# Expert weights of a mixture-of-experts block, read in runs of 4 KB a partition instead of 2 KB

## The chip, the core and the metric

One Trainium2 chip, and of it one core. The metric is the time of one execution on the device in microseconds (us); the kernel before takes 679.34 us in the median of three runs (679.24, 679.34 and 680.87). One further execution was profiled, and every row of a profile or trace in this text comes from that one.

## The reference

One layer of a hybrid encoder block on 512 tokens of width 1024, all in float32: a mixing part (attention and a state-space part), then a mixture of experts in two levels. The change lies in the second part:

```python
def hierarchical_moe(h, w_rg, b_rg, w_re, b_re, w1, w3, w2):
    ...
    for e in range(N_EXPERTS):                               # 16
        y_e = (jax.nn.silu(t @ w1[e]) * (t @ w3[e])) @ w2[e]
        out = out + combine[:, e:e + 1] * y_e
```

`w1[e]` and `w3[e]` are 1024 x 512, `w2[e]` is 512 x 1024, each 2 MB; the 48 matrices make 100.7 MB. `combine` is zero but for two experts a token, so an expert sees only its own tokens. Before the experts come the residual sum `x`, its norm and a router.

## The kernel before

**The mixing part** ends in a product with `w_out`, whose pieces `wt` are read, split into a high and a low half (ScalarE, VectorE) and multiplied into PSUM banks `px`. For each tile t of 128 tokens and each half nh of the width, VectorE adds the residual (`x2_add`, L1362), ScalarE squares it, TensorE turns it for the router, and `u_w` (L1400 to L1402) multiplies it by the norm's weights into `us`. `u_mul` scales `us` by 1/rms, and `h2_store` writes it to HBM as `h2_d`. Between the `u_w`s VectorE runs the router's top-k.

**The experts.** Each of 16 experts has 96 slots, in three rounds r of 32. The work goes in four quarters q: expert 4j+q has the 32-column strip j of TensorE, so that four experts run beside each other. A *group* is the four multiplies of one channel block k and one round r; each stands in the trace as two passes. The gathered tokens are turned to `TH` (channels on partitions); `up_mm` (L1671) multiplies eight blocks k of `w1` (phase "u") and of `w3` (phase "v"); `g_silu` (ScalarE) and `g_mul` (VectorE) make the gated product, `s_t` and `s_out` turn it, and `down_mm` (L1680) multiplies four blocks k of `w2`. The width of the result is done in two halves, phases "0" and "1", each with its own loads. `y_ev` weighs the result (VectorE for half 1, L1843), and GpSimd adds it to the output by an indirect DMA (`scatter`, L1709). In the last quarter the down groups go by r, then half, then k.

**The order.** `Plan` (L123) simulates the kernel on the host with a cost for each job, a due number (`prio`) and pools of buffers, and emits the instructions of each engine in the order that comes out; nothing is reordered on the chip. `phases` (L1739) sets the order of the experts' phases and loads.

**The loads.** All 192 come from the SP queue by `eload` (L1711), 512 KB each: two blocks k of one matrix of one expert, on 128 partitions. They go into 35 buffers, which `spent` gives back four at a time after the last round of a block pair. A load takes its channels as

```python
    w1v = w1[0].rearrange("e (k p) f -> e p k f", p=P)
```

so a partition holds channels p, 128 + p, ...: its two rows of a load lie apart in HBM, and each is a run of 512 x 4 B = 2 KB. A name such as 13_1_3 in a trace is half 1 of quarter 3, second pair of blocks, strip 3: it is the last load of all.

Of the kernel before, what the change touches and what calls it, by code (L numbers as in the profile page):

```python
# [15 lines left out]
AF = mybir.ActivationFunctionType  # L16
ALU = mybir.AluOpType
# [3 lines left out]
P = 128  # L21
# [7 lines left out]
DE = 512  # L29
# [185 lines left out]
def tile_block(ctx: ExitStack, tc: tile.TileContext, x, norm_mix_w, w_in, b_gate, q_norm_w, k_norm_w,  # L215
# [1179 lines left out]
    def u_rs(t):  # L1395
        tt = slice(t, t + 1)
        return [(0.07, lambda: V.scalar_tensor_tensor(ss2[:, tt], ssh[:, t, 0:1], EPS, ssh[:, t, 1:2], op0=ALU.add, op1=ALU.add))
                ] + rsqrt(rs2[:, tt], ss2[:, tt], 1, 0)

    def u_w(t, nh):  # L1400
        ns = slice(nh * 512, (nh + 1) * 512)
        V.tensor_tensor(us(t)[:, ns], x2(t)[:, ns], nfw()[:, ns], op=ALU.mult)  # L1402

    def u_mul(t):
        A.activation(us(t), us(t), AF.Copy, scale=rs2[:, t:t + 1])
# [172 lines left out]
    job("dve", 0.1, lambda: V.tensor_copy(cnt, t_["plt"][:, 144:160]), [j_, j_slot[NT - 1]], free=["ac"], prio=800)  # L1578


    w1v = w1[0].rearrange("e (k p) f -> e p k f", p=P)
    w3v = w3[0].rearrange("e (k p) f -> e p k f", p=P)
    w2v = w2[0].rearrange("e (k p) f -> e p k f", p=P)
    ohp = [cp.tile([P, NT, P], BF16, name="oh_%d" % i) for i in range(NR)]


# [93 lines left out]
    def down_mm(h, q, r, k, tag):  # L1680
        if k == 0:
            t_["p", h, q, r] = bank(tag, "py%s%d_%d" % (h, q, r))
        for j in range(4):
            js = slice(j * RN, (j + 1) * RN)
            T.matmul(t_["p", h, q, r][js, :], lhsT=sT_(r)[:, k, js], rhs=t_["raw", h, q, k // 2, j][:, k % 2, :],  # L1685
                     start=k == 0, stop=k == 3)

    def spent(x_, q, kk):

        for j in range(4):  # L1690
            t_.pop(("raw", x_, q, kk, j))
            ebufs.append(t_.pop(("buf", x_, q, kk, j), r4))

    def g_silu(q, r):
        A.activation(s_buf(r), t_["p", "u", q, r], AF.Silu)

    def g_mul(q, r):
        V.tensor_tensor(s_buf(r), s_buf(r), t_["p", "v", q, r], op=ALU.mult)  # L1698

    def s_t(q, r):  # L1700
        t_["ps", q, r] = bank("tp", "ps%d_%d" % (q, r))
# [14 lines left out]
    def source(x_, e, kk):  # L1716
        if x_ in "uv":
            return (w1v if x_ == "u" else w3v)[e][:, kk * 2:kk * 2 + 2, :]
        return w2v[e][:, kk * 2:kk * 2 + 2, int(x_) * 512:(int(x_) + 1) * 512]

    def more(make, nm, after):

# [12 lines left out]
    for i in range(2):  # L1735
        more(g8, "EXu%d" % i, j_h2[2 * i:2 * i + 2] + pgs)


    phases = [("u", 0), ("v", 0), ("u", 1), ("0", 0), ("1", 0), ("v", 1), ("u", 2), ("0", 1), ("1", 1), ("v", 2), ("u", 3),  # L1739
              ("0", 2), ("1", 2), ("v", 3), ("0", 3), ("1", 3)]  # L1740
    at = {ph: 2000 + 100 * i for i, ph in enumerate(phases)}
    jw, jT, jti, jsT, jy, jmul, jgx = {}, {}, {}, {}, {}, {}, {}
    for x_, q in phases:
        for kk in range(4 if x_ in "uv" else 2):
            for j in range(4):
                key = (x_, q, kk, j)
                jw[key] = last["e"] = job(
                    "dma", 1.38, lambda key=key: eload(key, source(key[0], 4 * key[3] + key[1], key[2])),
                    [j_rq] + ([last["e"]] if "e" in last else []), ["e"], prio=1000 + len(jw), lat=DLAT)

    def sl_jobs(q):
# [26 lines left out]

    def t_jobs(q):
        for r in range(NR):  # L1780
            o = (1900, at["v", 0] + 40 + 6 * r) [q] if q < 2 else at["0", q - 2] + 1 + r if r < 2 else at["v", q - 1] + 3
            jT[q, r] = []
            for kb in range(2):
                tk = ["T"] * (kb == 0)
                if (q, r) == (0, 0):
                    k_, free = pgj[kb], ["sc"]
                else:
                    k_ = [job("pe", 0.55, lambda r=r, kb=kb: t_mm(q, r, kb), [jgx[q, r]] + jT[q, r], ["tp"],
                              ["G"] if kb else [], prio=o + r, duty=0.5)]
                    free = ["tp"]  # L1790
                jT[q, r] = jT[q, r] + [job(
                    "dve" if kb else "act", 0.6 if kb else 0.48,
                    lambda r=r, kb=kb: t_out(q, r, kb, t_["pg", kb] if (q, r) == (0, 0) else t_["pg", q, r, kb]),
                    k_ + [j_rooms], tk, free, prio=o - 1500)]
# [24 lines left out]
                    jsT[q, r] = job("act", 0.48, lambda r=r: s_out(q, r), [k_], ["sT"], ["tp"], prio=p_)  # L1819
        return prev  # L1820

    def y_jobs(q, r, h, ks, tag, o, prev):
        end = ks[-1] == 3
        for k in ks:
            def f(k=k):
                down_mm(h, q, r, k, tag)
                if r == NR - 1 and k % 2:
                    spent(h, q, k // 2)
            prev = [job("pe", 0.857, f, [jw[h, q, k // 2, j] for j in range(4)] + [jsT[q, r]] + prev, [tag] if k == 0 else [],
                        (["e"] * 4 if r == NR - 1 and k % 2 else []) + (["sT"] if h == "1" and k == 3 else []), prio=o)]  # L1830
        if end:
            hi = int(h)
            jy[q, r, hi] = job("dve" if hi else "act", 0.6, lambda: y_ev(h, q, r, hi), prev + [jti[q][1]],
                               ["ys"] if hi == 0 else [], [tag], prio=o - 1500)
            if hi:
                k_ = job("pool", 1.03, lambda: scatter(q, r), [jy[q, r, 0], jy[q, r, 1]] + jsc[-1:], prio=o)
                jsc.append(job("dma", 1.3, lambda: None, [k_], free=["ys"], prio=-400, lat=6.0))
        return prev
# [14 lines left out]
    for x_, q in phases[2:]:  # L1853
        if x_ in "uv":
            prev = up_jobs(x_, q, prev)
        elif q < NQ - 1:
            tags = ("mm", "mm", "ac") if x_ == "1" else ("sc", "sc", "sc")
            for k in range(4):
                for r in range(NR):
                    prev = y_jobs(q, r, x_, [k], tags[r], at[x_, q] + k, prev)  # L1860
        elif x_ == "0":
            for r in range(NR):
                for h in "01":
                    prev = y_jobs(q, r, h, [0, 1, 2, 3], (("mm", "mm"), ("ac", "sc"), ("sc", "sc"))[r][int(h)], at["0", q] + 10 * r,
                                  prev)
    plan.run()
    order.close()

# [22 lines left out]
    def xround(e):  # L1891

        V.tensor_scalar(cur[:, 0:NT], cur[:, 0:NT], -float(CAP), None, op0=ALU.add)
        V.tensor_tensor(ohx, iota[:, :N].unsqueeze(1).to_broadcast([P, NT, N]),
                        cur[:, 0:NT].unsqueeze(2).to_broadcast([P, NT, N]), op=ALU.is_equal)
        pi = bank("ac", "pix")
        for t in range(NT):
            T.matmul(pi[:N, 0:5], lhsT=ohx[:, t, :], rhs=rcx[:, t, :], start=(t == 0), stop=(t == NT - 1))
        V.tensor_scalar(ixx[:N], pi[:N, 0:1], pi[:N, 1:2], None, op0=ALU.add)
        V.tensor_scalar(fxx[:N, 0:1], pi[:N, 0:1], pi[:N, 1:2], spare[:N, 0:1], op0=ALU.add, op1=ALU.subtract)  # L1900
        V.reduce_sum(fxx[:N, 1:2], pi[:N, 2:5], axis=AX.X)
        V.tensor_scalar(fxx[:N, 2:3], fxx[:N, 1:2], 0.0, None, op0=ALU.is_gt)
        V.tensor_tensor(fxx[:N, 0:1], fxx[:N, 0:1], fxx[:N, 2:3], op=ALU.mult)
        V.tensor_scalar(sxx[:N], fxx[:N, 0:1], spare[:N, 0:1], None, op0=ALU.add)
        g, tx, s_, sT, y_ = g_buf(0), T_(0, 0), s_buf(0), sT_(0), y_buf(0)
        gather(g[:N], ixx[:N, 0:1])

        def turn(src, dst, n, k0):
            pt = bank("tp", "ptx%d" % k0)
            for j in range(4):  # L1910
                T.transpose(pt[:, j * P:j * P + N], src[:N, (k0 + j) * P:(k0 + j + 1) * P], ident[:N, :N])
            A.activation(dst[:, k0:k0 + 4, :N], pt.rearrange(K4, k=4)[:, :, :N], AF.Copy)
        for k0 in (0, 4):
            turn(g, tx, N, k0)
        ex = [w[bass.ds(e, 1)].rearrange("o p k f -> p (o k) f") for w in (w1v, w3v, w2v)]

        def xpiece(nm, src):
            raw = r4(nm, F32, K8, k=2)
            nc.sync.dma_start(raw, src)
            return raw  # L1920

        def product(w_, lh, nk, cols, tag, nm):
            b_ = bank(tag, nm)
            for kk in range(nk // 2):
                raw = xpiece("%s_%d" % (nm, kk), w_[:, kk * 2:kk * 2 + 2, cols])
                for k in range(2):
                    T.matmul(b_[:N, :], lhsT=lh[:, kk * 2 + k, :N], rhs=raw[:, k, :], start=kk + k == 0,
                             stop=(kk + 1) * 2 == nk and k == 1)
            return b_
        A.activation(s_[:N], product(ex[0], tx, KD, slice(0, DE), "mm", "pux")[:N], AF.Silu)  # L1930
        V.tensor_tensor(s_[:N], s_[:N], product(ex[1], tx, KD, slice(0, DE), "mm", "pvx")[:N], op=ALU.mult)
        turn(s_, sT, N, 0)
        for h in range(2):
            hs = slice(h * 512, (h + 1) * 512)
            A.activation(y_[:N, hs], product(ex[2], sT, 4, hs, "sc", "pyx%d" % h)[:N], AF.Copy, scale=fxx[:N, 1:2])
        G.indirect_dma_start(out, bass.IndirectOffsetOnAxis(ap=sxx[:N, 0:1], axis=0), y_[:N], None, compute_op=ALU.add)
# [37 lines left out]
```

## Time and profile before

| | us |
|---|---|
| median of three runs | 679.34 |
| the profiled execution's own time | 680.03 |
| its span in the trace | 678.3 |
| first load of the experts issued | 270.68 |
| first multiply of the experts | 381.7 |
| first down group of the last quarter | 634.54 |
| last multiply ends (1.02 after 665.88) | 666.90 |

Times in the rows count from the span's start. Idle time stands in brackets behind an instruction, with what ended it. A busy TensorE is not one at its peak, since the ends of multiplies are modelled; its pace is read from the starts.

### The profile page before, as it was taken

The page shows a single profiled execution, that of the slowest core. Times are in us where ns is not written, and L with a number is a line of the kernel's source. Part 1 is how long each engine was busy: PE and PEld are TensorE (multiplying, and loading weights), DVE is VectorE, ACT ScalarE, POOL GpSimd, SP SyncE. Part 2 cuts the span into 40 slices and gives each one's busy share as a digit, 9 for nine tenths or more (in the row PEclk, how much of TensorE's full clock was granted, in tenths as well). Part 3 has the DMA queues.
Part 4 walks back from the last instruction along what each step waited for, and adds up shares of the span by engine and source line. Part 5 has one row for each costly group of instructions (what it writes and reads, how often), then busy time and mean ns, then how long its engine had stood idle before and what let it go on. Part 6 is the DMA issues. An engine that isn't in the chain of part 4 may idle for free. (4 is left out here: it accounts for less than half of the span.)

```text
span 678.3 us, 11450 instructions
## 1 busy us (share of the span) xinstructions
PE 653.3 (96%) x4635; PEld 396.6 (58%) x4637; DVE 321.2 (47%) x663; ACT 249.5 (37%) x450; POOL 84.2 (12%) x111
## 2 busy tenths in 40 slices
PE   7899999999999999999999999999999999999893
PEld 6788887777888888888877533323333333333220
DVE  4779868978699996666435731200110011001100
ACT  5535555777668778523435111111001100110100
POOL 4624100222000000000012110101200010001001
PEclk8999999999999999999999899999999999999997
DMA  8721733565221112997727959999999999999954
GB/s 283 192 75 42 178 94 71 155 180 128 61 63 35 30 33 66 279 359 258 268 103 277 345 174 386 390 388 390 364 340 388 388 363 337 388 386 363 340 143 64
DMA packets 104189, 155.37 MB, mean 229 GB/s; under 512 B 8569, under 2 KB 44933, under 8 KB 104133
## 3 DMA queue, kind: packets, MB, share of 16 engines
q1 hardware_dynamic: 95268, 131.79, 56.8%
q0 software_dynamic: 6800, 22.76, 12.8%
q8 instruction: 37, 0.61, 0.4%
q10 hardware_dynamic: 2064, 0.07, 0.2%
q14 instruction: 20, 0.16, 0.1%
HBM read 144.01 MB, written 10.58 MB: 228 GB/s over the span
## 5 line engine op out<-in xcount | busy, mean ns | idle before, releaser
L268 PE MATMUL b<-hTh,wc_hi 128*128 128x512 f32 x208 | 84.5, 406 | 0.0
L270 PE MATMUL b<-hTh,wc_lo 128*128 128x512 f32 x208 | 81.3, 391 | 0.0
L269 PE MATMUL b<-hTl,wc_hi 128*128 128x512 f32 x208 | 81.3, 391 | 0.0
L1677 PE MATMUL pu<-u,TH 128*32 128x512 f32 x528 | 63.8, 597 | 0.0
L1677 PE MATMUL pv<-v,TH 128*32 128x512 f32 x372 | 58.9, 593 | 0.0
L1843 DVE TENSOR_SCALAR YS<-py,ti 128x512 f32<-128x512 f32 x12 | 9.0, 751 | 89.4 <-PE py L1685 89.0
L1667 DVE COPY TH<-pg 128x512 f32<-128x512 f32 x12 | 8.3, 692 | 90.8 <-PE pg L1662 90.0
L1706 ACT ACTIVATE GS<-ps 128x512 f32<-128x512 f32 x12 | 7.0, 601 | 111.0 <-PE ps L1703 111.0
L663 ACT ACTIVATE wc_hi<-wc_r 128x1024 fp32r<-128x1024 f32 x34 | 36.0, 1059 | 29.3 <-PE b L269 22.2
L667 DVE TENSOR_TENSOR wc_lo<-wc_r,wc_hi 128x1024 fp32r<-128x1024 f32 x34 | 41.5, 1222 | 7.4 <-ACT wc_hi L663 7.3
L268 PEld LDWEIGHTS b<-hTh,wc_hi 128*128 128x128 f32 x208 | 39.1, 188 | 9.7 <-issue 1.5
L270 PEld LDWEIGHTS b<-hTh,wc_lo 128*128 128x128 f32 x208 | 39.0, 188 | 8.6
L269 PEld LDWEIGHTS b<-hTl,wc_hi 128*128 128x128 f32 x208 | 39.1, 188 | 7.1
L1677 PEld LDWEIGHTS pu<-u,TH 128*32 128x32 f32 x528 | 18.0, 111 | 38.8 <-issue 37.5
L1709 POOL DMA_INDIRECT out_dram<-YS,sx x12 | 18.7, 1562 | 145.0 <-DVE YS L1843 79.4
L1677 PEld LDWEIGHTS pv<-v,TH 128*32 128x32 f32 x372 | 15.4, 110 | 29.9 <-issue 29.8
L1677 PE MATMUL pv<-EXr,TH 128*32 128x512 f32 x96 | 32.7, 595 | 0.0
L1669 ACT ACTIVATE TH<-pg 128x512 f32<-128x512 f32 x12 | 7.2, 597 | 67.8 <-PE pg L1662 65.1
L1698 DVE TENSOR_TENSOR YS<-YS,pv 128x512 f32<-128x512 f32 x8 | 5.5, 689 | 46.0 <-PE pv L1677 46.0
L1677 PE MATMUL pv<-EXx,TH 128*32 128x512 f32 x120 | 26.8, 593 | 0.0
L1656 POOL DMA_INDIRECT GS<-h_d,ix x11 | 10.7, 970 | 122.0 <-PE pg L1662 111.9
L1163 DVE TENSOR_TENSOR PTl<-ppt,PTh 128x512 fp32r<-128x512 f32 x32 | 21.6, 687 | 4.4 <-ACT PTh L1158 4.2
(451 smaller groups left out, 1708.4 us busy)
## 6 DMA issues: line engine op xcount, KB each, us to landing
u<-in_w_dram SPq DMA_DIRECT2D x44, 512.0 KB
v<-in_w_dram SPq DMA_DIRECT2D x31, 512.0 KB
wc_r<-in_w_in_dram SPq DMA_DIRECT2D x26, 512.0 KB
EXx<-in_w_dram SPq DMA_DIRECT2D x20, 512.0 KB
EXr<-in_w_dram SPq DMA_DIRECT2D x20, 512.0 KB
EXu<-in_w_dram SPq DMA_DIRECT2D x20, 512.0 KB
EXm<-in_w_dram SPq DMA_DIRECT2D x10, 512.0 KB
x<-in_x_dram SPq DMA_DIRECT2D x8, 512.0 KB
```

The source lines that it names most:

```text
L268: T.matmul(ps, lhsT=lh, rhs=rh, start=first, stop=False)
L269: T.matmul(ps, lhsT=lh, rhs=rl, start=False, stop=False)
L270: T.matmul(ps, lhsT=ll, rhs=rh, start=False, stop=last)
L663: A.activation(t_["w", i][0], t_["raw", i], AF.Copy)
L667: V.tensor_tensor(l_, t_.pop(("raw", i)), h_.bitcast(F32), op=ALU.subtract)
L1163: V.tensor_tensor(PTl[:, :, q2], t_.pop(("pt", u)).rearrange("p (k q) -> p k q", k=NT), PTh[:, :, q2].bitcast(F32), op=ALU.subtract)
L1656: G.indirect_dma_start(g, None, h2_d, bass.IndirectOffsetOnAxis(ap=i, axis=0))
L1667: V.tensor_copy(o, i)
L1669: A.activation(o, i, AF.Copy)
L1677: T.matmul(t_["p", x_, q, r][js, :], lhsT=T_(q, r)[:, k, js], rhs=t_["raw", x_, q, k // 2, j][:, k % 2, :], start=k == 0, stop=k == KD - 1)
L1709: G.indirect_dma_start(out, bass.IndirectOffsetOnAxis(ap=sx[q][:, r:r + 1], axis=0), y_buf(r), None, compute_op=ALU.add)
L1843: V.tensor_scalar(o, i, w_, None, op0=ALU.mult)
```

## The change

The channels of `w1` and `w3`, and the gated products that `w2` takes, are numbered "(p k)" instead of "(k p)". A partition then holds neighbouring channels, and the two rows that it takes in one load are one run of 4 KB. To match, `u_w` writes the tokens' channels in the new order (its inputs are read eight elements, 32 B, apart), and `g_silu` and `g_mul` read their PSUM banks four elements (16 B) apart. The down loads take one block k of the full width of 1024 instead of two blocks of a half, so phases "0" and "1" become one phase "w", in which each block serves both halves. The planner's cost of a load is 1.29 instead of 1.38. The path for experts with more than 96 tokens, which the trace does not run, follows suit.

```diff
     def u_w(t, nh):
         ns = slice(nh * 512, (nh + 1) * 512)
-        V.tensor_tensor(us(t)[:, ns], x2(t)[:, ns], nfw()[:, ns], op=ALU.mult)
+        by_k = lambda a: a[:, ns].rearrange("n (p k) -> n k p", k=KD)
+        V.tensor_tensor(us(t).rearrange("n (k p) -> n k p", k=KD)[:, :, nh * 64:nh * 64 + 64], by_k(x2(t)), by_k(nfw()), op=ALU.mult)
...
-    w1v = w1[0].rearrange("e (k p) f -> e p k f", p=P)
-    w3v = w3[0].rearrange("e (k p) f -> e p k f", p=P)
-    w2v = w2[0].rearrange("e (k p) f -> e p k f", p=P)
+    w1v = w1[0].rearrange("e (p k) f -> e p k f", p=P)
+    w3v = w3[0].rearrange("e (p k) f -> e p k f", p=P)
+    w2v = w2[0].rearrange("e (p k) f -> e p k f", p=P)
...
-            T.matmul(t_["p", h, q, r][js, :], lhsT=sT_(r)[:, k, js], rhs=t_["raw", h, q, k // 2, j][:, k % 2, :],
+            T.matmul(t_["p", h, q, r][js, :], lhsT=sT_(r)[:, k, js],
+                     rhs=t_["raw", "w", q, k, j].rearrange("p a n -> p (a n)")[:, int(h) * 512:(int(h) + 1) * 512],
                      start=k == 0, stop=k == 3)
...
+    def by_k(a):
+        return a.rearrange("n (p k) -> n k p", k=4)
+
     def g_silu(q, r):
-        A.activation(s_buf(r), t_["p", "u", q, r], AF.Silu)
+        A.activation(s_buf(r).rearrange("n (k p) -> n k p", k=4), by_k(t_["p", "u", q, r]), AF.Silu)
 
     def g_mul(q, r):
-        V.tensor_tensor(s_buf(r), s_buf(r), t_["p", "v", q, r], op=ALU.mult)
+        s_ = s_buf(r).rearrange("n (k p) -> n k p", k=4)
+        V.tensor_tensor(s_, s_, by_k(t_["p", "v", q, r]), op=ALU.mult)
...
-        return w2v[e][:, kk * 2:kk * 2 + 2, int(x_) * 512:(int(x_) + 1) * 512]
+        return w2v[e][:, kk:kk + 1, :].rearrange("p k (a n) -> p (k a) n", a=2)
...
-    phases = [("u", 0), ("v", 0), ("u", 1), ("0", 0), ("1", 0), ("v", 1), ("u", 2), ("0", 1), ("1", 1), ("v", 2), ("u", 3),
-              ("0", 2), ("1", 2), ("v", 3), ("0", 3), ("1", 3)]
+    phases = [("u", 0), ("v", 0), ("u", 1), ("w", 0), ("v", 1), ("u", 2), ("w", 1), ("v", 2), ("u", 3), ("w", 2), ("v", 3), ("w", 3)]
...
-                    "dma", 1.38, lambda key=key: eload(key, source(key[0], 4 * key[3] + key[1], key[2])),
+                    "dma", 1.29, lambda key=key: eload(key, source(key[0], 4 * key[3] + key[1], key[2])),
...
-        elif q < NQ - 1:
-            tags = ("mm", "mm", "ac") if x_ == "1" else ("sc", "sc", "sc")
-            for k in range(4):
-                for r in range(NR):
-                    prev = y_jobs(q, r, x_, [k], tags[r], at[x_, q] + k, prev)
-        elif x_ == "0":
-            for r in range(NR):
-                for h in "01":
-                    prev = y_jobs(q, r, h, [0, 1, 2, 3], (("mm", "mm"), ("ac", "sc"), ("sc", "sc"))[r][int(h)], at["0", q] + 10 * r,
-                                  prev)
+        else:
+            ks = [(k, h, r) for k in range(4) for h in "01" for r in range(NR)]
+            tags = (("sc", "mm"), ("sc", "mm"), ("sc", "ac"))
+            if q == NQ - 1:
+                ks.sort(key=lambda o_: (o_[2], o_[1]))
+                tags = (("mm", "mm"), ("ac", "sc"), ("sc", "sc"))
+            for n, (k, h, r) in enumerate(ks):
+                prev = y_jobs(q, r, h, k, tags[r][int(h)], at[x_, q] + n, prev)
```

How the order of instructions moves is shown at three places. The first is TensorE around the last load, in round 0 of the last quarter. Before (py_0_5580 is half 1 of round 0, py_1_5598 the first bank of round 1):

```order
L1685 MATMUL py_0_5580<-13_1_2_5567,GS_3665 32x512
L1685 MATMUL py_0_5580<-13_1_3_5578,GS_3665 32x512
L1685 MATMUL py_0_5580<-13_1_0_5537,GS_3665 32x512
L1685 MATMUL py_0_5580<-13_1_1_5549,GS_3665 32x512
L1685 MATMUL py_0_5580<-13_1_2_5567,GS_3665 32x512
L1685 MATMUL py_0_5580<-13_1_3_5578,GS_3665 32x512
L1685 MATMUL py_1_5598<-03_0_0_5414,GS_3665 32x512
```

The last load holds blocks 2 and 3 of half 1: two groups use it before round 1. After the change (py_0_5556 is half 0 of round 0, w_3_3 the last load):

```order
L1687 MATMUL py_0_5556<-w_2_3_5441,GS_3665 32x512
L1687 MATMUL py_0_5556<-w_3_0_5456,GS_3665 32x512
L1687 MATMUL py_0_5556<-w_3_1_5466,GS_3665 32x512
L1687 MATMUL py_0_5556<-w_3_2_5472,GS_3665 32x512
L1687 MATMUL py_0_5556<-w_3_3_5482,GS_3665 32x512
L1687 MATMUL py_0_5580<-w_0_0_5346,GS_3665 32x512
L1687 MATMUL py_0_5580<-w_0_1_5352,GS_3665 32x512
```

The last load is now met in half 0, with the four groups of half 1 (py_0_5580) still to come before round 1.

The second place is SP while the last pieces of the mixing part are read (wc_r, the last of eight; wt_r, w_out). Before:

```order
L1714 DMA u_2_0_3053<-in_w_dram 128x2x512
L656 DMA wc_r_3064<-in_w_ssd_o_dram 128x4x128
L657 DMA wc_r_3064<-in_w_attn_o_dram 128x4x128
L1714 DMA u_2_1_3067<-in_w_dram 128x2x512
L1714 DMA u_2_2_3087<-in_w_dram 128x2x512
```

After:

```order
L1722 DMA u_2_0_3048<-in_w_dram 128x1024
L1722 DMA u_2_1_3059<-in_w_dram 128x1024
L656 DMA wc_r_3066<-in_w_ssd_o_dram 128x4x128
L657 DMA wc_r_3066<-in_w_attn_o_dram 128x4x128
L1722 DMA u_2_2_3073<-in_w_dram 128x1024
```

One load of an expert moves ahead of wc_r, and in the same way one ahead of the first two pieces wt_r; a partition's two runs (2x512) are now one (1024).

The third is VectorE at the first `u_w`s, where the order stays and the form changes (one piece of the difference):

```order
 L1362 TENSOR_TENSOR x_0_3297<-x_0_3297,px_1_3264 128x512
-L1402 TENSOR_TENSOR us_3395<-x_0_3297,lp_3257 128x512 x2
+L1404 TENSOR_TENSOR us_3395<-x_0_3297,lp_3257 128x8x64 x2
 L1362 TENSOR_TENSOR x_1_3300<-x_1_3300,px_2_3273 128x512
-L1402 TENSOR_TENSOR us_3418<-x_1_3300,lp_3257 128x512
+L1404 TENSOR_TENSOR us_3418<-x_1_3300,lp_3257 128x8x64
```

Nothing else moves among the `u_w`s or the router's steps.

## Rows read from the trace of the kernel before

**Rows 1.** The page: the span, gigabytes a second in 40 slices of it, a DMA queue.

```profile
span 678.3 us, 11450 instructions
...
GB/s 283 192 75 42 178 94 71 155 180 128 61 63 35 30 33 66 279 359 258 268 103 277 345 174 386 390 388 390 364 340 388 388 363 337 388 386 363 340 143 64
...
q10 hardware_dynamic: 2064, 0.07, 0.2%
```

**Rows 2.** A stretch of 50 us: length, TensorE busy, granted clock, DMA share, GB/s.

```profile
600.00:650.00 50.00, 46.54 (x377) 1.00 1.03 354
```

**Rows 3.** SP in order of time: issues of a wc_r, of x, and of loads 36 to 47, 49, 177, 192.

```profile
292.12 0.37 SPq L656 DMA_DIRECT2D wc_r<-in_w_ssd_o_dram  x1
...
320.87 2.33 SPq L1318 DMA_DIRECT2D x<-in_x_dram  x4
...
403.31 8.78 SPq L1714 DMA_DIRECT2D u<-in_w_dram  x12
...
414.40 0.58 SPq L1714 DMA_DIRECT2D 00_0_0_4139<-in_w_dram  x1
...
613.13 0.63 SPq L1714 DMA_DIRECT2D 03_0_0_5414<-in_w_dram  x1
...
640.23 1.13 SPq L1714 DMA_DIRECT2D 13_1_3_5578<-in_w_dram  x1
```

**Rows 4.** TensorE in order of time: load 49's first use, then the last quarter's down phase.

```profile
455.34 0.59 PE L1685 MATMUL py<-00_0_0_4139,GS 128*32 128x512 f32 x1
...
634.54 0.59 PE L1685 MATMUL py<-03_0_0_5414,GS 128*32 128x512 f32 x1
...
635.39 0.59 PE L1685 MATMUL py<-03_0_0_5414,GS 128*32 128x512 f32 x1
...
636.37 0.66 PE L1703 MATMUL ps<-cst,GS 128*128 128x128 f32 x4
...
641.28 1.05 PE L1685 MATMUL py<-13_0_0_5497,GS 128*32 128x512 f32 x2 [1.23 <-DMA 13_0_0_5497<-in_w_dram]
...
651.26 0.62 PE L1685 MATMUL py<-13_1_3_5578,GS 128*32 128x512 f32 x1 [0.28 <-SPq L1938]
...
665.88 1.02 PE L1685 MATMUL py<-13_1_3_5578,GS 128*32 128x512 f32 x2
```

**Rows 5.** Short stretches, columns as rows 2: only x moves (first three), only experts' loads (last two).

```profile
326.00:327.00 1.00, 1.00 (x6) 1.00 1.02 397
327.00:328.00 1.00, 1.00 (x6) 1.00 1.03 418
328.00:329.00 1.00, 1.00 (x6) 1.00 1.02 401
...
444.00:448.00 4.00, 4.00 (x40) 1.00 1.05 387
...
593.00:597.00 4.00, 4.00 (x40) 1.00 1.05 387
```

**Rows 6.** VectorE in order of time: a split, u_w, a wait, a plain and a strided product.

```profile
341.28 1.22 DVE L1339 TENSOR_TENSOR wt_lo<-wt_r,wt_hi 128x1024 fp32r<-128x1024 f32 x1
...
369.83 0.69 DVE L1402 TENSOR_TENSOR us<-x,lp 128x512 f32<-128x512 f32 x1
...
374.81 0.24 DVE L1414 SCALAR_TENSOR_TENSOR lp<-plt,rs,prm 128x20 f32<-128x20 f32 x1 [0.86 <-PE plt L1393]
...
380.76 0.22 DVE L1496 TENSOR_TENSOR cw<-cw,lp 128x64 f32<-128x64 f32 x1
...
383.11 0.27 DVE L1499 TENSOR_TENSOR lp<-cw,rc 128x64 f32<-128x64 f32 x1
```

**Rows 7.** TensorE's use of that split; ScalarE's first use of the wc_r of rows 3; a silu.

```profile
346.65 0.40 PE L269 MATMUL px<-wt_lo,mTh 128*128 128x512 f32 x1
...
305.68 1.06 ACT L663 ACTIVATE wc_hi<-wc_r 128x1024 fp32r<-128x1024 f32 x1 [3.18 <-DMA u<-in_w_dram]
...
454.73 0.60 ACT L1695 ACTIVATE YS<-pu 128x512 f32<-128x512 f32 x1 [0.26 <-PE pu L1677]
```

More of the change, by code (lines that the diff above doesn't have):

```diff
@@ L1743, in tile_block @@
     for x_, q in phases:
-        for kk in range(4 if x_ in "uv" else 2):
+        for kk in range(4):
             for j in range(4):
@@ L1780, in t_jobs @@
         for r in range(NR):
-            o = (1900, at["v", 0] + 40 + 6 * r) [q] if q < 2 else at["0", q - 2] + 1 + r if r < 2 else at["v", q - 1] + 3
+            o = (1900, at["v", 0] + 40 + 6 * r) [q] if q < 2 else at["w", q - 2] + 1 + r if r < 2 else at["v", q - 1] + 3
             jT[q, r] = []
@@ L1820, in up_jobs, with y_jobs, f @@
         return prev
[L1822 to L1831, printed above, removed]
+    def y_jobs(q, r, h, k, tag, o, prev):
+        end = (r, h) == (NR - 1, "1")
+        def f():
+            down_mm(h, q, r, k, tag)
+            if end:
+                spent("w", q, k)
+        prev = [job("pe", 0.857, f, [jw["w", q, k, j] for j in range(4)] + [jsT[q, r]] + prev, [tag] if k == 0 else [],
+                    (["e"] * 4 if end else []) + (["sT"] if h == "1" and k == 3 else []), prio=o)]
+        if k == 3:
             hi = int(h)
@@ L1929, in product @@
             return b_
-        A.activation(s_[:N], product(ex[0], tx, KD, slice(0, DE), "mm", "pux")[:N], AF.Silu)
-        V.tensor_tensor(s_[:N], s_[:N], product(ex[1], tx, KD, slice(0, DE), "mm", "pvx")[:N], op=ALU.mult)
+        sk = s_[:N].rearrange("n (k p) -> n k p", k=4)
+        A.activation(sk, by_k(product(ex[0], tx, KD, slice(0, DE), "mm", "pux")[:N]), AF.Silu)
+        V.tensor_tensor(sk, sk, by_k(product(ex[1], tx, KD, slice(0, DE), "mm", "pvx")[:N]), op=ALU.mult)
         turn(s_, sT, N, 0)
```

## The prediction

> **What bounds the kernel now.** I read the page first, then the stretches, and then SP and TensorE in order of time; the chain of waits names only the tail. On the page the GB/s slices fall apart in two [rows 1]: up to the middle the DMA engines are mostly idle, and from slice 25 on, the experts, they stand at 340 to 390 to the end. The stretch from 600 to 650 us [rows 2] shows both engines at work, TensorE 46.5 of 50 us at a granted clock of 1.00, the DMA at a share of 1.03. Two engines that look full cannot both be the bound, and the order in time tells which is. Load 49 is issued at 414.40 [rows 3] and first used at 455.34 [rows 4], 40.9 us ahead. Load 177 is issued at 613.13 and used at 634.54, 21.4 ahead. Load 192, the last, is issued at 640.23 and used at 651.26, the moment it lands. So loads pass at one in (613.13 - 414.40) / 128 = 1.553 us, gathers and scatters included, while TensorE uses them at one in (634.54 - 455.34) / 128 = 1.400. TensorE lives on a stock that runs out just before the end. Until then the DMA queue's slowness costs nothing; in the last quarter's down phase the waits appear, as at 641.28, where the multiply waited for its DMA [rows 4].
>
> What that costs: two passes from 634.54 to 635.39 make a group of 0.857 us (34 passes of 0.43 between 651.26 and 665.88). The down phase of the last quarter is 24 groups and four transposes (0.66), so without waits it would end at 634.54 + 20.6 + 0.7 + 0.2 (the last pass's run-out) = 656.0. It ends at 665.88 + 1.02 = 666.9. **10.9 us** is all that faster loads can give, since ahead of 634.54 TensorE waits for hardly any.
>
> **The loads.** 192 loads lose half their runs. Those up to 35 fill buffers that wait for other things; from load 36, at 403.31, twelve leave in 8.8 us as buffers come free, and after that SP is never short of one (35 buffers against 11 to 41 us of stock). So 157 loads count.
> With 2 KB runs the rate is 387 GB/s in both stretches where nothing else moves [rows 5], that is 524,288 B / 387,000 = 1.355 us a load. The nearest row for 4 KB runs is the four loads of x at 320.87 [rows 3]: while they alone move, 397, 418 and 401 GB/s, mean 405, or 1.294 us. There the DMA share is 1.02 and not 1.05, so the queue was less deep and 405 is rather low. A second way: packets of some 34 B (0.07 MB in 2064) take 0.2% of 16 engines' span [rows 1], 0.002 x 16 x 678.3 / 2064 = 10.5 ns each, nearly all of it a packet's own cost. A 2 KB packet at 387 GB/s and share 1.05 takes 16 x 2048 x 1.05 / 387,000 = 88.9 ns; two less one such cost are 5.9% less, or 1.275 us a load. I take 1.28, nearer the second since it holds at full depth: **0.075 us a load, 157 x 0.075 = 11.8 us**. The ends are 418 GB/s (0.101 a load, 15.8 us) and 397 (0.034, 5.3 us). No row has runs that lie 16 KB apart; the down loads (pitch 4 KB, 593 to 597) and the up loads (pitch 2 KB, 444 to 448) run alike at 387, so pitch has shown no price, but below nothing stays possible.
>
> The last load then lands at 651.26 - 11.8 = 639.5. Pitch with gathers becomes 1.553 - 0.075 = 1.478, still over TensorE's 1.400, so the stock still shrinks and buffers never hold SP back.
>
> **The order of the last quarter.** Before, the last load is used by two groups of half 1 and then by the 16 of rounds 1 and 2: from its landing to the last multiply's end 18 x 0.857 + 0.2 = 15.6, as the rows say (651.26 to 666.9). After, it is met in half 0: one group, four of half 1 and 16, 21 x 0.857 + 0.2 = 18.2 us. This is a loss of three groups, 2.6 us, which falls due as long as the landing and not TensorE sets the end. The end is the later of 639.5 + 18.2 = **657.7** and the floor of 656.0, which has no wait: 9.2 us earlier than 666.9.
>
> **The strided reads.** `u_w` (0.69 us, eight of them [rows 6]) reads two inputs 32 B apart. Bounds: nothing, and the excess of the strided product L1499 over the plain L1496, 0.05 us on 64 elements, so 0.4 us on 512. Four of them stand ahead of the last `wt_lo` split (341.28 to 342.5), which TensorE uses at 346.65 [rows 7]: 4.1 us of cover against 1.6. The last one, at 369.83, holds up the top-k of tile 2, and VectorE then waits 0.86 us for TensorE ahead of tile 3: 0.4 fits. Uncovered, it would add its 0.4 to all that follows. I take 0.
> By the Trainium skill ("SBUF — State Buffer", section on door 1, the note on cachelines) a read that moves to another 16-byte line at each element pays, and so does PSUM beyond 8 bytes; L1499, whose elements lie 16 B apart, agrees in sign, and with 0.4 us or with double the time (0.7) the sum would stay, by the same cover.
> The silu of the last round (0.60, [rows 7]) frees the bank that the first round-2 group of half 1 wants; that now comes 5 groups after the up phase (4.3 us) instead of 14. Three silus at double length would end 2.2 us after it. `g_mul` and `s_out` of the last quarter stand behind waiting loads. 0 for both.
>
> **SP's order in the mixing part.** One load moves ahead of `wc_r`: 1.3 us later for a piece issued at 292.12 and first used at 305.68. The DMA share of time it needs is a tenth of those 13.6 us: 0, and the `wt` pieces alike.
>
> **Sum.** 680.03 - 9.2 = 670.8 for the profiled execution; the median is 0.7 below it, so **670.1**. The tail from the last multiply to the end (678.3 - 666.9 = 11.4) and the 1.7 outside the span stay.
>
> **Rivals.**
> *Only part of the rate comes.* At the lowest of the 4 KB rows, 397 GB/s, the landing is 651.3 - 5.3 = 645.9, the end 664.1, the gain 2.8: 676.5. For it: one row in three. Against: share 1.02 there. The Trainium skill ("DMA: Bandwidth & Descriptors", "Why small descriptors are slow") gives about three cycles a packet beside 64 for 2 KB, an estimate of 2% for halving the packets; by that rule 677. The 10.5 ns of the small packets speaks for more.
> *Slower: the runs give nothing and the order costs.* If 4 KB runs at 16 KB pitch move no faster, the landing stays at 651.26 and the three groups are lost: 651.3 + 18.2 = 669.5, 2.6 us more, 682.0. It decides below 2.6 / 157 = 0.017 us a load, 1.2%; a rate under 387 makes it worse. For it: no row has this pitch. Against: rows 5.
> *TensorE becomes the bound.* At 418 GB/s the landing is 635.4, and the floor of 656.0 holds: 680.0 - 10.9 - 0.7 = 668.4.
> *Strided reads come through* at double length without cover: under 2 us later, 672.
> *The change does not do what it says*, since a run is still cut at 2 KB: the same 682.0. Against: the load has one run of 1024 now, the form in which x is read.
>
> **How the numbers follow.** Forecast with the floor at its fast end (gain 5.3 to 10.9, 668.4 to 674.0): 0.72. Part of the rate: 0.12. Strided reads: 0.05. Slower by either rival: 0.07 and 0.04. 0.3% is 2.0 us, about what a measurement can tell from no change. Faster: 0.72, nearly all of the part and of the strided, 0.84; same 0.07, from the part and the lightest of the slower cases; slower 0.09. The range runs from 668.0 (the floor, and a little for scatter of runs) to 676.5 (part of the rate), which leaves out the slower cases and some of the part, under 2 in 10.
>
> **What would show it.** In the changed trace: 400 to 415 GB/s where only loads move; the last load's first use near 639.5, waits only in front of it, the last multiply ending near 657.7; stock at load 177 near 31 us (21.4 + 128 x 0.075); `u_w` of 0.7 to 1.1 us with TensorE's first expert multiply still near 381.7. A rate of 387 or less, a first multiply later by over 1 us, or waits for PSUM banks in the w phases would make it wrong.

## The result, and the profile after

Median of 6 runs each: 670.06 us (669.12 to 670.64) against 680.44 (679.24 to 681.29). The ratio is 0.9848, with an interval from 0.9834 to 0.9862: 10.4 us faster. The forecast was 670.1. The profiled execution took 669.12 us, with a span of 667.3, against 680.03 and 678.3: 10.9 us. It is the fastest of the six, so the 10.4 us of the medians measure the gain better.

The page, to be laid beside [rows 1]:

```profile
span 667.3 us, 11451 instructions
...
GB/s 288 194 76 37 187 78 81 139 210 127 65 64 32 32 33 64 205 362 306 293 83 216 313 256 323 409 407 409 401 359 383 408 408 352 383 408 399 358 102 65
```

From slice 25 on the plain slices read 407 to 409 where they read 386 to 390, in a span that is 11.0 us shorter. The same two short stretches as in [rows 5], in which only experts' loads move (columns: stretch, length, TensorE's busy time, granted clock, DMA share, GB/s):

```profile
444.00:448.00 4.00, 4.00 (x44) 1.00 1.03 406
593.00:597.00 4.00, 4.00 (x42) 1.00 1.03 410
```

SP in order of time, for loads 36, 49, 177 and 192 as in [rows 3]:

```profile
402.68 10.96 SPq L1722 DMA_DIRECT2D u<-in_w_dram  x13
...
414.49 1.60 SPq L1722 DMA_DIRECT2D w<-in_w_dram  x2
...
603.16 22.39 SPq L1722 DMA_DIRECT2D w<-in_w_dram  x16
...
625.22 0.33 SPq L1722 DMA_DIRECT2D w<-in_w_dram  x1
```

From load 49 to load 177 the pitch is (603.16 - 414.49) / 128 = 1.474 us, where it was 1.553. Now TensorE and VectorE in order of time, the last quarter's down phase as in [rows 4]; the last row is VectorE's product that starts as the last multiply ends (it started at 666.94 before):

```profile
633.33 1.90 PE L1687 MATMUL py<-w,GS 128*32 128x512 f32 x16
...
635.75 20.22 PE L1687 MATMUL py<-w,GS 128*32 128x512 f32 x176
```

```profile
656.01 0.75 DVE L1850 TENSOR_SCALAR YS<-py,ti 128x512 f32<-128x512 f32 x1 [6.12 <-PE py L1687]
```

The waits of [rows 4], 1.23 us and shorter, are gone from this view. One is left that is too short for it: the fourth strip of the fourth group, which needs load 192, starts 0.68 us after the multiply ahead of it (637.06 to 637.75), where 0.43 is the rule. The chain of waits begins at that very multiply:

```profile
637.75 0.01 issue
637.75 4.49 PE py L1687 x37
```

So load 192 is first used at **637.75** (651.26 before), and from there to the last multiply's end it is 656.01 - 637.75 = **18.26 us**, the prediction's 21 groups and 0.2.

### The profile page after: what moved, and what is told of

It is laid out like the page before. It is cut to its first block, busy times and chain, and to the rows that moved or that the text cites. A ratio compares the mean times of both kernels' runs of the same rounds, so it can differ in the third digit from the quotient of the medians.

```text
span 667.3 us, 11451 instructions
## 1 busy us (share of the span) xinstructions
PE 645.5 (97%) x4636; PEld 394.4 (59%) x4637; DVE 324.3 (49%) x663; ACT 249.5 (37%) x450; POOL 83.5 (13%) x111
## 5 line engine op out<-in xcount | busy, mean ns | idle before, releaser
L1687 PE MATMUL py<-w,GS 128*32 128x512 f32 x564 | 64.4, 593 | 0.1
L1687 PEld LDWEIGHTS py<-w,GS 128*32 128x32 f32 x564 | 18.3, 110 | 38.3 <-issue 35.1
L1852 ACT ACTIVATE YS<-py,ti 128x512 f32<-128x512 f32 x12 | 8.3, 688 | 58.6 <-PE py L1687 43.4
```

Of the source, the lines that this page charges most:

```text
L1852: A.activation(o, i, AF.Copy, scale=w_)
```

## The experiments

In the diffs, "-" is the changed kernel and "+" the experiment. "Landing" of a load is read from the completion marks among the DMA packets of the trace; before, load 192 lands at 650.78, in the changed kernel at 637.22.

**Runs cut to 2 KB, two ways.** The first keeps everything of the change, the new channel order too, and takes apart only the runs:

```diff
 def source(x_, e, kk):
     if x_ in "uv":
-        return (w1v if x_ == "u" else w3v)[e][:, kk * 2:kk * 2 + 2, :]
+        return (w1v if x_ == "u" else w3v)[e][:, kk:kk + 5:4, :]
-    return w2v[e][:, kk:kk + 1, :].rearrange("p k (a n) -> p (k a) n", a=2)
+    i, j = (2 * kk, 2 * kk + 3) if kk < 3 else (1, 6)
+    return w2v[e].rearrange("p k (a n) -> p (k a) n", a=2)[:, i:j + 1:j - i, :]
```

(`up_mm` and `down_mm` pick the stationary blocks to match.)

> The changed kernel with every expert load cut back into two runs of 2 KB a partition (an up load takes channels k and k + 4 of a partition's eight, a down load half a row of one channel and the other half of another); loads, their number and order, phases, TensorE's order and strided reads stay as changed. Theory (the gain is the run length alone, through the landing of the last load): loads pass at 1.36 us again and not at 1.28, the last lands 156 x 0.08 = 12.5 us later than the changed kernel's 637.2, is first used at about 650.2, and with the 21 groups behind it the last multiply ends at 650.2 + 18.2 = 668.4: 12.4 later than in the changed kernel, 682.5, so 2 us slower than the kernel before. Rival (the gain is from the merged phases, the planner's constant or the channel order): 670, the rate unchanged at 407 to 410 GB/s or the landing without effect. Rival (the distance of the runs matters too): a rate that is not the 387 GB/s of before.

Measured: 690.01 us against 679.57, ratio 1.0136 (1.0099 to 1.0172). The gain needs the runs, so the first rival is out, but the theory missed by 7.5 us: load 192 landed at 661.35 and not at 649.7. (The profiled execution, 693.24 us, is the slowest of the four, so some 3 us of this lateness are its own.) The stretches show where (columns: stretch, length, granted clock, DMA share, GB/s), first those of this kernel, then of the kernel before:

```profile
444.00:448.00 4.00, 1.00 1.04 387
593.00:597.00 4.00, 1.00 1.05 387
...
405.00:425.00 20.00, 1.00 0.99 327
605.00:645.00 40.00, 1.00 1.03 330
```

```profile
405.00:425.00 20.00, 1.00 1.04 383
605.00:645.00 40.00, 1.00 1.05 357
```

Where loads have long run alone it is 387 again; after the burst at 403 and among the scatters it is far under the kernel before. One packet in a hundred takes over 328 ns there (405 to 425; 96 ns before), at the same median of 84 to 85. So the second rival, that the distance of the runs matters too, holds in these two stretches, and this kernel is no clean test of the run length; the next but one is.

The second edit is the order of the last quarter's groups, on top of the first:

```diff
-                ks.sort(key=lambda o_: (o_[2], o_[1]))
+                ks.sort(key=lambda o_: (o_[2], o_[1] if o_[2] else "", o_[0]))
```

> The same with one more edit: in the last quarter's down phase round 0 takes both halves of a channel block before the next block, so that 2 + 16 = 18 groups and not 1 + 4 + 16 = 21 stand behind the last load. Theory (the three groups are due when the landing sets the end): the last multiply ends 3 x 0.857 = 2.6 us sooner than in the kernel with cut runs and the changed order, 665.8, or 679.9 in all, with the same landing. Rival (the order of the groups costs nothing, other waits fill in): the same 682.5.

Measured: 688.65, ratio 1.0135 (1.0098 to 1.0172). It is 8.7 us over the 679.9 expected, since it inherits the miss of the first, and too close to the first to be told apart by the totals. The traces tell them apart: from the last landing to the last multiply's end it is 680.14 - 661.35 = 18.8 us with the changed order and 674.95 - 658.73 = 16.2 with this one, the 2.6 us of three groups.

**The order alone, and half of the runs each.** Here the channel order of before comes back, with its plain reads; phases, order and constant stay as changed. A down load joins halves of two channels that are 128 apart:

```diff
-    w1v = w1[0].rearrange("e (p k) f -> e p k f", p=P)
+    w1v = w1[0].rearrange("e (k p) f -> e p k f", p=P)
...
-        return w2v[e][:, kk:kk + 1, :].rearrange("p k (a n) -> p (k a) n", a=2)
+        i, j = (2 * kk, 2 * kk + 3) if kk < 3 else (1, 6)
+        at_ = lambda n: (n // 2) * P * D + n % 2 * 512
+        v = w2v[e]
+        return bass.AP(v.tensor, v.offset + at_(i), [[D, P], [at_(j) - at_(i), 2], [1, 512]])
```

> The order alone: phases, TensorE's order, loads' order and planner's constant as changed, but the channel order of before (so plain reads) and 2 KB runs in all loads; a down load takes half a row of one channel and the other half of a channel 128 on. Theory (no rate gain, three groups more behind the last load): loads at 1.36 us, the last lands within 1 us of the 650.8 of before, the last multiply ends at 651.3 + 18.2 = 669.5, 2.6 later: 682.2. Rival (what made the run with cut runs 7.5 us slower than expected lies in the order and not in its 16 KB pitch): 688 to 690.

Measured: 683.27 against 680.58, ratio 1.0031 (1.0016 to 1.0047): 2.7 us **slower** than before, where 2.6 was expected. (The total is 1.1 over 682.2, since the kernel before, run beside it, is 1.2 over the median from which that was worked out.) Load 192 lands at 650.70. TensorE and VectorE in order of time:

```profile
641.82 5.11 PE L1686 MATMUL py<-w,GS 128*32 128x512 f32 x8 [1.90 <-DMA w<-in_w_dram]
...
651.21 9.22 PE L1686 MATMUL py<-w,GS 128*32 128x512 f32 x84 [0.27 <-SPq L1944]
```

```profile
669.46 0.75 DVE L1851 TENSOR_SCALAR YS<-py,ti 128x512 f32<-128x512 f32 x1 [6.12 <-PE py L1686]
```

The waits for loads are those of before, the first use is at 651.21, and 18.25 us follow it where 15.68 did (666.94 - 651.26). In the two long stretches it moves what the kernel before does (columns: stretch, length, granted clock, DMA share, GB/s):

```profile
405.00:425.00 20.00, 1.00 1.04 386
605.00:645.00 40.00, 0.97 1.05 357
```

So the packets that dragged on in the first experiment belong to where its 2 KB runs lie (8 KB apart, in a pitch of 16 KB) and not to the order.

Down loads alone in runs of 4 KB (whole rows in the old channel order, 4 KB pitch; all else as in the kernel of the order alone):

```diff
-    w2v = w2[0].rearrange("e (p k) f -> e p k f", p=P)
+    w2v = w2[0].rearrange("e (k p) f -> e p k f", p=P)
...
     return w2v[e][:, kk:kk + 1, :].rearrange("p k (a n) -> p (k a) n", a=2)
```

> The same, but the down loads read whole rows (4 KB runs, 4 KB pitch, the channel order of before); up loads stay at 2 KB. Theory (each load gains by itself): 64 of the 157 loads gain 0.08 us, 5.1 in all; last landing 645.7, end of the last multiply 664.4, 677.1. Rival (the gain needs all loads or the 16 KB pitch): 682.

Measured: 678.53 against 680.58, ratio 0.9975 (0.9962 to 0.9987); landing 645.96.

```profile
646.43 13.94 PE L1686 MATMUL py<-w,GS 128*32 128x512 f32 x128 [0.21 <-SPq L1941]
```

```profile
664.68 0.75 DVE L1848 TENSOR_SCALAR YS<-py,ti 128x512 f32<-128x512 f32 x1 [6.12 <-PE py L1686]
```

Landing and end lie within 0.3 us of what was expected, and 18.25 us stand again between the first use and the end. The total is 1.4 over 677.1, most of it again the slower kernel before. Now the up loads alone, read as changed (`w1v` and `w3v` of the change, `u_w` strided), while the down loads have the source of the order alone:

> The other half: up loads as changed (4 KB runs, 16 KB pitch, u_w strided), down loads at 2 KB in the old channel order. Theory: 93 loads gain 0.08 us, 7.4 in all; last landing 643.4, end of the last multiply 662.1, 674.8. Rival (the pitch of 16 KB costs the up loads part of it): between 675 and 682.

Measured: 678.07 against 680.58, ratio 0.9962 (0.9948 to 0.9976); landing 644.57, VectorE's last product at 663.79. That is 6.1 us ahead of the order alone where 7.4 were expected (7.0 at the step of 0.076 us a load that the next experiment shows), and 5.7 at the end. The total is 3.3 over the theory's 674.8 and lies in the rival's range. Of that, 1.2 us are the slower kernel before and 0.4 the 0.08 taken for 0.076; of the rest, some 1.5 us, 0.4 can be the strided `u_w` (see the strided reads below). What remains has no cause here, and that it is a price of the pitch in this kernel is not ruled out. The two halves give 5.7 and 4.8 us at the last multiply's end; together they give 669.46 - 656.01 = 13.45. Some of the surplus is traffic that falls behind the last landing (next section); 1 to 2 us of it stay without a cause.

**The rate by itself.** A kernel of weight loads alone, 16.8 MB in each of seven patterns:

> Leaves out the whole computation: SP alone reads the experts' weights, up to eight loads in flight, 16.8 MB in each of seven patterns one after the other: up and down loads as before (2 KB runs), up loads with 2 KB runs 8 KB apart in a pitch of 16 KB, up loads as changed (4 KB runs, 16 KB pitch), down loads of whole rows in the old channel order (4 KB runs, 4 KB pitch), then runs of 8 KB and of 16 KB. Theory (a packet costs about 10 ns of its own, (1.36 - 1.28) us over the 8 packets that a load saves on each of 16 engines): 387 GB/s at 2 KB, 408 to 410 at 4 KB whatever the pitch, 423 at 8 KB, 430 at 16 KB. Rival (pitch matters): the two 4 KB patterns differ by over 1%. Rival (2 KB runs 8 KB apart are slow by themselves, as the run with cut runs suggests): the third pattern under 380. Rival (the gain ends at 4 KB): 8 and 16 KB at 408 to 410.

One execution; the stretches in the order of the patterns (columns: stretch, length, VectorE, GpSimd, clock, DMA share, GB/s):

```profile
12.00:42.00 30.00, 0.00 (x0) 0.00 (x0) 1.00 1.05 388
55.00:85.00 30.00, 0.00 (x0) 0.00 (x0) 1.00 1.05 387
98.00:128.00 30.00, 0.00 (x0) 0.00 (x0) 1.00 1.05 384
140.00:165.00 25.00, 0.00 (x0) 0.00 (x0) 1.00 1.03 410
180.00:205.00 25.00, 0.00 (x0) 0.00 (x0) 1.00 1.03 410
222.00:245.00 23.00, 0.00 (x0) 0.00 (x0) 1.00 1.01 422
260.00:280.00 20.00, 0.91 (x1) 0.00 (x0) 1.00 1.01 428
```

2 KB runs: 388, 387 and, 8 KB apart, 384. 4 KB runs: 410 at a pitch of 16 KB and 410 at 4 KB. 8 and 16 KB: 422 and 428. All three rivals are out for a steady stream of loads: run length sets the rate, pitch changes nothing at 4 KB and 1% at 2 KB, and the rate goes on rising past 4 KB.

**Does the landing or TensorE set the end now?** The order edit above, on the changed kernel with its 4 KB runs:

> The changed kernel, 4 KB runs, with only that order of round 0 in the last quarter. Theory (TensorE has become the bound: in the changed kernel the one wait ahead of the last load's first use is 0.25 us): the last multiply ends at most 0.3 us before 656.0, 669.7 to 670.1 in all. Rival (the landing still sets the end as the prediction's sum had it, 1.7 us over the floor): 1.7 us sooner, 668.4.

Measured: 669.33 against 679.57, ratio 0.9842 (0.9812 to 0.9872). The total decides for neither side: its last multiply ends at 656.36, but its last down phase began 1.45 us later than in the changed kernel. Then the same with down loads in whole rows of the old channel order, so that silu and `g_mul` read plain; and, beside it, the changed kernel once more.

> The changed kernel with two edits: round 0 of the last quarter takes both halves of a channel block before the next (as in the run that had this alone), and the down loads read whole rows in the old channel order (4 KB runs, 4 KB pitch), so that silu and g_mul read plain again; up loads and u_w as changed. Theory (TensorE is the bound, so only the wait ahead of the last loads can go): no wait in the last down phase, its start plus 21.6 us is the last multiply's end; 0 to 1.1 us under the changed kernel of the same call. Rival (strided silu and g_mul delayed something): over 1.5 us under it.

> The changed kernel as it is, once more beside the two others of this call, to compare within a percent. All theories: the ratio to the kernel before that it had, 0.983 to 0.986. Theory (the landing still sets its end, by some 1 us over what TensorE needs): the last multiply's end is the first use of the last load plus 18.2.

Measured against 680.30: 669.51, ratio 0.9838 (0.9820 to 0.9855), and the changed kernel 670.02, ratio 0.9847 (0.9831 to 0.9863). None of the three can be told from another by its total. The traces can: this is the kernel with both edits, TensorE and then VectorE.

```profile
634.72 1.90 PE L1687 MATMUL py<-w,GS 128*32 128x512 f32 x16
637.14 19.09 PE L1687 MATMUL py<-w,GS 128*32 128x512 f32 x176
```

```profile
656.30 0.75 DVE L1849 TENSOR_SCALAR YS<-py,ti 128x512 f32<-128x512 f32 x1 [6.12 <-PE py L1687]
```

Its last down phase takes 656.30 - 634.72 = 21.58 us, and with the order edit alone 656.36 - 634.78 = 21.58 too. The changed kernel takes 656.01 - 633.33 = 22.68, and in its second profile 655.23 - 632.93 = 22.30. So 21.58 is the phase without a wait; in the changed kernel the landing still sets the end, by 0.7 to 1.1 us (its second profile first uses load 192 at 636.98, and 18.25 us follow), and behind it stands TensorE. That lies between the theory (0.3 at most) and the rival (1.7). In these executions the phase of the two edited kernels began 1.4 to 1.9 us later, for a reason that lies ahead of the experts (last section), and load 192 landed later with it (638.31 and 638.52), so that the microsecond which the order freed does not show in the totals.

**The strided reads.** `u_w`, silu and `g_mul` in plain order (`g_mul` edited like silu):

```diff
-        V.tensor_tensor(us(t).rearrange("n (k p) -> n k p", k=KD)[:, :, nh * 64:nh * 64 + 64], by_k(x2(t)), by_k(nfw()), op=ALU.mult)
+        V.tensor_tensor(us(t)[:, ns], x2(t)[:, ns], nfw()[:, ns], op=ALU.mult)
...
-        A.activation(s_buf(r).rearrange("n (k p) -> n k p", k=4), by_k(t_["p", "u", q, r]), AF.Silu)
+        A.activation(s_buf(r), t_["p", "u", q, r], AF.Silu)
```

> The changed kernel with u_w, g_silu and g_mul reading and writing in plain order (channels then stand in another order than the weights', so the expert part computes with mismatched channels); loads and order as changed. Theory (all strided reads are covered): u_w falls from 1.11-1.18 to 0.69 us, eight times 0.45, the first expert multiply and the last multiply's end move by less than 0.4 us: 669.7 to 670.2. Rival (they hold up TensorE): the first expert multiply up to 3.6 us sooner, and with it the end, 666.5 to 668.5.

Measured: 669.27 against 679.57, ratio 0.9840 (0.9811 to 0.9869); the changed kernel has 0.9848 and 0.9847. The totals can't tell a microsecond; the traces can. The durations of the changed kernel, by line (line, engine, form, count, busy, mean ns of one):

```profile
L1404 DVE TENSOR_TENSOR us<-x,lp 128x512 f32<-128x512 f32 x8 | 9.1, 1154 | 0.1
L1706 DVE TENSOR_TENSOR YS<-YS,pv 128x512 f32<-128x512 f32 x8 | 5.5, 688 | 46.0 <-PE pv L1679 46.0
L1702 ACT ACTIVATE YS<-pu 128x512 f32<-128x512 f32 x8 | 4.8, 604 | 42.9 <-PE pu L1679 42.9
```

`u_w` takes 1.15 us for 0.69, 8 x 0.46 = 3.7 us more on VectorE. How much of it reaches TensorE is read from VectorE in order of time, at the last `u_w`, ahead of tile 3's top-k; first the kernel before (its `u_w` and its last row stand in [rows 6]), then the changed one:

```profile
369.11 0.69 DVE L1362 TENSOR_TENSOR x<-x,px 128x512 f32<-128x512 f32 x1 [0.17 <-PE px L270]
```

```profile
368.55 0.69 DVE L1362 TENSOR_TENSOR x<-x,px 128x512 f32<-128x512 f32 x1 [0.17 <-PE px L270]
369.27 1.11 DVE L1404 TENSOR_TENSOR us<-x,lp 128x512 f32<-128x512 f32 x1
...
374.66 0.24 DVE L1416 SCALAR_TENSOR_TENSOR lp<-plt,rs,prm 128x20 f32<-128x20 f32 x1 [0.86 <-PE plt L1393]
```

From the residual add to tile 3's first step it is 374.81 - 369.11 = 5.70 us before and 374.66 - 368.55 = 6.11 after. It is 5.70 in all four executions with a plain `u_w` and 6.11 to 6.12 in all eight with a strided one, and the wait of 0.86 us for TensorE stays as long. So the last `u_w` passes its 0.41 us on to the router's steps and the first expert multiply. The seven ahead of it are covered: from the first `u_w` to the start of the last it is 33.1 us in all kernels with the changed order, strided or plain (32.8 in the kernel before). The first expert multiply alone, one start of each kernel (380.10 with plain reads, 380.58 and 380.35 in the changed kernel), would not have told, since it scatters by more (last section). silu and `g_mul` take what they took, 0.604 and 0.688 (0.689 before), though they read PSUM 16 B apart.

**The planner's constant.**

```diff
-                    "dma", 1.29, lambda key=key: eload(key, source(key[0], 4 * key[3] + key[1], key[2])),
+                    "dma", 1.38, lambda key=key: eload(key, source(key[0], 4 * key[3] + key[1], key[2])),
```

> The changed kernel with the planner's cost of a load at 1.38 as before: three loads of the mixing part stand elsewhere in SP's order, nothing else moves. Theory: within 0.7 us of the changed kernel of the same call. Rival (the new constant is part of the gain): 1 us or more above it.

Measured: 669.74 against 680.30, ratio 0.9841 (0.9825 to 0.9857), the changed kernel 0.9847 beside it. It has no part in the gain.

## Why the prediction was right

**The bound** was right: the DMA queue is the slower of two nearly full engines and is paid for only at the end. The stock at load 177 was to be 31 us and is 633.33 - 603.16 = 30.2.

**The rate** was right. 1.28 us a load was taken and 0.075 saved; 410 GB/s is 1.279, and the step from 387 to 410 is 0.076. The choice of the second way over the mean of the rows of x (405) is borne out by the kernel of loads alone, as is what it rested on, a cost of each packet's own: their mean durations there are 88, 163, 314 and 615 ns for 2, 4, 8 and 16 KB, that is 75 ns for each 2 KB and 13 more. The Trainium skill ("DMA: Bandwidth & Descriptors", "Why small descriptors are slow") gives three cycles a packet, by which halving the packets was worth 2%, an estimate; the rows differ, with 5.9%, and decide. One reading of the prediction is wrong without consequence: in both of its stretches of 2 KB runs only down loads move (from 444 to 448 they are loads 61 to 64, by the order of the loads), and no up loads. But from 451 to 465, where the 2 KB up loads of quarter 1 land, it is 386 GB/s too.

**The landing** was the term that was off: 639.5 forecast, first use at 637.75, so 13.5 us earlier and not 11.8. The step that was off is "The last load then lands at 651.26 - 11.8": it takes it that all gathers and scatters which stood ahead of the last load still do. (The pitch up to load 177 came as forecast, 1.474 for 1.478.) But no scatter waits for a load: the first of a quarter waits for VectorE's product, and so for TensorE's groups, and the later ones follow 10 to 11 us apart. GpSimd's third scatter of quarter 2 before, then the first and the third after:

```profile
633.39 1.55 POOL L1709 DMA_INDIRECT out_dram<-YS,sx  x1 [9.12 <-ACT GS L1706]
```

```profile
611.32 1.55 POOL L1717 DMA_INDIRECT out_dram<-YS,sx  x1 [43.44 <-DVE YS L1850]
...
632.71 1.55 POOL L1717 DMA_INDIRECT out_dram<-YS,sx  x1 [9.15 <-DMA out_dram<-YS,sx]
```

Before, all of it passed ahead of load 192; after, the loads have overtaken part of it. Between the landings of loads 36 and 192 the software queue, which carries them, moves 8.12 MB where it moved 8.39: 67 packets of 4 KB at a median of 0.327 us on 16 engines, 1.4 us. With 0.4 us by which load 36 lands sooner (406.21 against 406.58) that is the 1.8, within what these readings can tell. The 0.4 us are luck: load 36 follows the start of the experts, which scatters (last section). The second profile of the changed kernel bears the rest out: 8.06 MB, and 13.6 us less from landing 36 to landing 192, where the first has 13.2.

**The order of the last quarter** was right to a tenth: 18.2 us after the first use of the last load, and 18.26, 18.25 and 18.25 in three kernels; the order alone costs 2.7 us, 2.6 by the sum.

**The end** was to be the later of 657.7 and the floor of 656.0. Measured: 656.01, still set by the landing, 1.1 us over a floor that itself came lower, 633.33 + 21.58 = 654.9; that it equals the floor of the forecast is chance. Had the landing come 1.1 us sooner still, the rival in which TensorE becomes the bound would have been the case. The sum gave 9.2 us for the profiled execution and 10.9 came; the medians give 10.4, and the landing's 1.8 us are the difference in the first. So that the forecast of 670.1 and the median of 670.06 agree is luck as well: the gain came out 1.2 us larger than the sum, and the kernel before, measured beside, 1.1 us slower than the median that the sum began with.

**The strided reads** were covered but for one. The step "VectorE then waits 0.86 us for TensorE ahead of tile 3: 0.4 fits" is wrong: the wait is still 0.86 us with the strided read, what it waits for has moved with it, and the last `u_w` delays the first expert multiply by 0.41 us. The term that was put at 0 should have been 0.4, the price that the prediction itself gave for an uncovered read (measured, 0.42 to 0.5 us each, against its upper bound of 0.4). Whether all of it reaches the end, the totals are too coarse to show; in the six kernels with 4 KB runs throughout, load 192 lands 255.8 to 256.6 us after the first expert multiply, which speaks for it. The Trainium skill ("SBUF — State Buffer", section on door 1, the note on cachelines) lets a read pay that moves to a new 16-byte line at each element; the trace agrees, with 1.15 us for 0.69. For PSUM it gives lines of 8 bytes and speaks of slower matmuls; silu and `g_mul`, with 0.604 and 0.688 us, show no price for 16 B. **SP's order** cost nothing, as the planner's constant shows.

**The rivals.** Part of the rate: out, by 410 GB/s. The runs still cut at 2 KB: out by the same row, and the order alone shows what it would have been, 683.3 where 682.0 was worked out from a median that lay 1.2 lower. The runs that give nothing at 16 KB pitch: out for 4 KB runs. TensorE as the bound: 1.1 us short of it. Strided reads that come through: 0.41 us of one, as said.

## What to carry to other kernels

A queue that is slower than its consumer but starts with a stock costs only at the end, so price a faster queue there: the landing of the last load, plus the work that needs it, against the consumer's own time without waits. Count the groups behind the last load whenever an edit reorders them; here three groups, 2.6 us, weigh as much as the gain of 34 loads, and an order written in one line gives them back when they are due. Before summing a per-transfer saving, look at what else shares the DMA engines and what sets its time: it may fall behind the end and make the saving larger, or the reverse. A wait after a step that gets slower is no cover for it, unless what is waited for goes on without that step.

## What the runs showed that was not expected

2 KB runs 8 KB apart in a pitch of 16 KB move at 384 GB/s alone, like any others, and at 327 to 330 after a burst or among scatters, where other 2 KB runs hold 357 to 386; a few packets then take several times the median. What holds them up was not tried. The 4 KB runs of the change show a trace of it (one packet in a hundred over 281 ns in 405 to 425), worth well under 1 us.

The first expert multiply starts anywhere from 380.1 to 382.7 us in twelve executions of these kernels. The last residual add, 11.6 to 13.2 us ahead of it, scatters by 1.9 us, from 368.3 to 370.3, for a reason that was not sought. The strided `u_w` adds 0.41. The rest is TensorE's clock; the kernel before, then the changed one (columns: stretch, length, TensorE's busy time, granted clock, DMA share, GB/s):

```profile
379.00:382.00 3.00, 3.00 (x27) 0.57 1.01 377
```

```profile
379.00:382.00 3.00, 3.00 (x38) 1.00 1.02 380
```

Before, the clock stood at the lower of its two levels, 1.2 GHz, for most of these 3 us, and in the changed kernel at the upper; yet in the 3 us ahead TensorE was busy alike, 1.32 and 1.33 us. From tile 3's first step on VectorE to the first expert multiply it is 5.92 us in the six executions without such a fall and 6.37 to 7.03 in the six with one, so it costs 0.4 to 1.1 us. The kernel with both edits is among the first six and began its experts at 382.28 because its last residual add came late (370.25). These are one or two microseconds that, but for the 0.41, no edit here chose, as much as separates the best of these kernels.
